# One layer of an mLSTM and convolution trunk: two weight splits moved to VectorE, a norm spread by transfers, another PSUM layout, and edits at both ends

## The chip, the cores and the metric

The kernel runs on one core of a Trainium2 chip. The metric is the device time of one execution in microseconds (us), as the median of three runs. Engines are named as in the profile: PE is TensorE, DVE is VectorE, ACT is ScalarE, POOL is GpSimd, SP is SyncE.

## The reference, cut to what matters

One layer is computed for 128 context tokens and 512 latent tokens of 1024 channels, all in fp32:

```
mod  = silu(cond) @ w_ada + b_ada            # six vectors: shift, scale, gate, twice
h    = rmsnorm(x) * (1 + sc1) + sh1
q, k, v, o, gates, u, ga, gb = split(h @ w_in + b_in)
hA   = bidirectional_mlstm(q, k, v, gates)    # 4 heads, chunks of 128 tokens
branch_a = (sigmoid(o) * norm(hA)) @ w_proj_a
z    = depthwise_conv31(ua * sigmoid(ub))     # 512 channels
branch_b = silu(layernorm(z)) @ w_proj_b      # mean and variance over the 512 channels
x    = x + g1 * ((sigmoid(ga) * branch_a + sigmoid(gb) * branch_b) @ w_out)
h2   = rmsnorm(x) * (1 + sc2) + sh2
gate, val = split(h2 @ w_up)                  # 2 x 2816 columns
x    = x + g2 * ((gelu(depthwise_conv(gate)) * val) @ w_down)
y    = rmsnorm(x)
```

## The kernel before, in words

**Layout.** Channels lie on the 128 partitions and the 640 tokens along a row, so `x` is eight tiles of 128x640. A product with a weight block of 128x128 is done as two matmuls of 320 tokens. An fp32 product is made of three products of a rounded format: weights and activations are each split into a high part and a remainder (`wh`, `wl` for weights; `hh`, `hl` or `ah`, `al` for activations), and TensorE adds wh·hh, wh·hl and wl·hh.

**Weights.** They come in groups of eight blocks, 512 KB each, into a ring of three tiles `wst`, by transfers that SyncE issues. `prep` (line 474) splits a group: ScalarE writes `wh`, and then `wl` comes about in one of two ways. For most groups VectorE computes `wl = wst - wh` (L491). For the groups in the set `TWICE` (line 163) ScalarE writes -`wh` into `wl`, and a transfer issued on GpSimd's queue adds the weights to it from DRAM (L486 to L488). `wh` and `wl` have three tiles each, and from the middle of the up-projection on there is a third ring of three, `wf`.

**Order.** Nothing runs in the order of the text. A planner in the kernel (`_Order`) keeps a cost estimate for every engine and writes one fixed instruction order for each; every instruction is recorded by its helper at line 182 (line 183 in the changed kernel), so the rows of the profile are told apart by tiles. Work is kept in side tasks and in lanes that `od.later` fills and the planner draws from when VectorE seems free: the taps of the convolutions, and the rows `junk`, which compute the six modulation vectors (each multiplies a 128x512 tile `ad` of `w_ada` by the condition, the sum lands in `modp`). `od.need(tag)` writes out at once whatever is left in a lane. The engines run their orders with semaphores between them.

**Stages**, in the order of PE: modulation and first norm; the input projection in the order of `ORDER` (u0 g0 k0 q0 k1 q1 u1 v0 u2 u3 k2 q2 k3 q3 v1 o0 to o3), with the small products of the mLSTM scan, two heads at a time, among them; the two gates and two branch projections in the order of `BRANCH`; the output projection `woA`, `woB`; up- and down-projection; the last norm.

**The convolution's norm** (`conv_norm`, line 1260). When the taps of the four tiles `z` (128x656) are done, 16 products with a tile of ones add up the channels: the sums of the 656 columns come to lie as 4 rows of 164. VectorE scales them to the mean `mu`, `bcast` (line 670) spreads the 4 rows over all partitions with four products `ps<-mu,sel`, VectorE subtracts half a tile at a time, ScalarE squares (`zsq`), 16 more products add up the squares, a short chain on 128x164 gives `rsy`, and `bcast` spreads it by `ps<-rsy,sel`. `conv_out` (line 1294) multiplies and applies the activation; the first branch projection of z is b0.

**PSUM** has eight banks. `psum_pools` (line 393) opens the pool `mm` for the projections and the pool `ps` for small products, anew just before b0 with six banks for `mm` and two for `ps` (line 1397). Tiles of the two are recorded as `mm` and `ps`. In this kernel `mm` then has banks 0 to 5.

**Down-projection and last modulation vector.** In the loop over the tiles f of the up-projection (line 1733) the down-projection runs in parts; a part (`dn_part`, line 1714) has four outputs, and each is added to `x` by VectorE with the gate vector g2 (`x<-mm,mods,x`). Before the first part, at f = 4 (`min(DN_AT)`), stands:

```
        if not wf and (not od.waits("g2") or f == min(DN_AT)):
            od.need("g2")
            g2_in.append(True)
            last.close()
            wf.append(ctx.enter_context(tc.tile_pool(name="wf", bufs=NWF)))
```

`last.close()` frees the tiles `ad`, and `wf` takes their memory: the first ScalarE writes to `wf` wait for the last `junk` to have read.

**The last norm** (`final`, line 1746). The tokens of the second part (256) take squares, sums over channels by products with ones (4 rows of 64 columns), the chain `rsy`, `rsv`, `rst` on 128x64, four spreading products, eight multiplications `yo`, and the last stores.

Of the kernel before, what the change touches and what calls it, by code (L numbers as in the profile page):

```python
# [20 lines left out]
T = NCTX + NLAT  # L21
# [5 lines left out]
TF = 656  # L27
# [49 lines left out]
TL = 384  # L77
# [71 lines left out]
GB = 8  # L149
BLOCKS, HELD, PAIRS = _blocks()  # L150
# [212 lines left out]
def tile_trunk(  # L363
# [17 lines left out]
    od = _Order()  # L381
    V, S, G, PE, Q, GQ = (_Timed(e, od, k) for e, k in ((nc.vector, "V"), (nc.scalar, "S"), (nc.gpsimd, "G"),
                                                        (nc.tensor, "PE"), (nc.sync, "Q"), (nc.gpsimd, "R")))
# [6 lines left out]
    pools = {}  # L390

    def psum_pools(nmm, nps, banks):
        if pools:
            pools["stack"].close()
        pools["stack"] = st = ExitStack()
        pools["nmm"], pools["nps"], pools["banks"] = nmm, nps, banks
        od.rings.clear()
        pools["mm"] = st.enter_context(tc.tile_pool(name=f"mm{nmm}", bufs=nmm, space=bass.MemoryType.PSUM))
        pools["ps"] = st.enter_context(tc.tile_pool(name=f"ps{nps}", bufs=nps, space=bass.MemoryType.PSUM))

    psum_pools(2, 4, 2)
    ctx.enter_context(tc.manual_schedule())
    first, last = ExitStack(), ctx.enter_context(ExitStack())
    adp = first.enter_context(tc.tile_pool(name="adp", bufs=2 * NAD1))

    def A(shape, dt=F32, name="a"):
        return ap.tile(shape, dt, tag="A", name=name)
# [18 lines left out]
    def ps():  # L426
        return od.ring("ps", pools["ps"].tile([P, 512], F32, tag="ps", name="ps"), pools["nps"])
# [2 lines left out]
        return t[:, 0:T].rearrange("p (h n) -> p h n", h=2)  # L430

    HALF = [slice(0, TH), slice(TH, T)]


    cols = cp.tile([P, NCOLS], F32, name="cols")
    sel = cp.tile([P, NSEL], F32, name="sel")
    ident = sel[:, 0:128]
# [15 lines left out]
    lines = {}  # L453
# [17 lines left out]
    def wtile(tag):  # L471
        return od.ring(tag, (wf[0] if tag == "wf" else wp).tile([P, GB * P], F32R, tag=tag, name=tag), CAPS[tag])

    def prep(g, tags=("wh", "wl")):


        if g in ready or g >= NGRP:
            return
        load(g)
        src = stage.pop(g)  # L480
        tag_of["c", g, 0] = tags
        hi, lo = wtile(tags[0]), wtile(tags[1])

        def parts():
            yield from od.until(src)
            S.activation(hi, src, AF.Copy)  # L486
            if g in TWICE:
                S.activation(lo, src, AF.Copy, scale=-1.0)  # L488
                live.pop(g)
                GQ.dma_start(lo, w_d[g], accum_op=ALU.add)  # L490
                return  # L491
            yield
            V.tensor_sub(lo, src, hi.bitcast(F32))
            live.pop(g)

        ready[g] = (hi, lo)
        lines[g] = od.spawn(parts())
# [161 lines left out]
    ones32 = cp.tile([P, 32], F32, name="ones32")  # L659
    V.memset(ones32, 1.0)  # L660
    epsc = cp.tile([P, 1], F32, name="epsc")
    V.memset(epsc, EPS)
    bgrp = T // 4

    def colsum_into(pc, tile_, n, first, last):
# [4 lines left out]
    def bcast(r, n):  # L670
        out = []
        for h in range(2):
            pt = ps()
            for j in range(2):
                g = 2 * h + j
                PE.matmul(pt[:, j * n:(j + 1) * n], lhsT=sel[:, 256 + g:257 + g].to_broadcast([P, P]), rhs=r,
                          start=True, stop=True)
            out.append(pt[:, 0:2 * n])
        return out

    def rstd(src, w, scale, name):

# [17 lines left out]
    x = []  # L700
    for j in range(KD):
        t = A([P, T], name="x")
# [21 lines left out]
    pc = ps()  # L724
    for j in range(KD):
        sq = A([P, T], name="sq")
        S.activation(sq, x[j], AF.Square)
        if j == 3:
            th = small([P, 16], "th")
            S.activation(th, colr("c"), AF.Tanh, scale=0.5)  # L730
            sqrt_table()
        colsum_into(pc, sq, bgrp, j == 0, j == KD - 1)
# [11 lines left out]
    for nm in ("b_ua", "b_ub", "b_o", "mlstm_g", "ln_g", "ln_b", "b_ga", "b_gb"):  # L744
        a, b = _COLS[nm]
# [2 lines left out]
        o += b - a  # L748

    r1 = rstd(pc[:, 0:bgrp], bgrp, 1.0 / D, "rs")  # L750
    prep(0)

    def hcol(name, i):
        return halfc[:, HC[name] + i:HC[name] + i + 1]
# [51 lines left out]
    t_ada = od.spawn(ada1())  # L806
    while not mrows:
        od.finish_one()
    rb = bcast(r1, bgrp)
    t = A([P, T], name="rbs")  # L810
    for h in range(2):
# [40 lines left out]
    z = [None] * 4  # L852
# [91 lines left out]
    for p in range(2):  # L944
        for c in range(NCH):
            t = vp.tile([P, 2, P1], F32, tag="v", name="va")
# [310 lines left out]
    nz = TF // 4  # L1257
    zs = {}

    def conv_norm():  # L1260
        while len(conv_in) < 4 or od.waits("conv"):
            yield
        yield from od.until(*z)
        pc = ps()
        for m in range(4):
            colsum_into(pc, z[m], nz, m == 0, m == 3)
        mu = small([P, nz], "mu")
        V.tensor_scalar(mu, pc[:, 0:nz], 1.0 / 512, None, op0=ALU.mult)
        yield
        mb = bcast(mu, nz)  # L1270
        pc = ps()
        sqs = []
        for m in range(4):
            for h in range(2):
                s = slice(2 * nz * h, 2 * nz * (h + 1))
                V.tensor_sub(z[m][:, s], z[m][:, s], mb[h])
            sq = A([P, TF], name="zsq")
            S.activation(sq, z[m], AF.Square)
            sqs.append(sq)
        for m in range(4):  # L1280
            yield from od.until(sqs[m])
            colsum_into(pc, sqs[m], nz, m == 0, m == 3)
        rz = rstd(pc[:, 0:nz], nz, 1.0 / 512, "rs")
        yield
        rb = bcast(rz, nz)
        ts_ = []
        for m in range(4):
            yield from od.room("V")
            ts_.append(od.spawn(conv_out(m, rb)))
            yield  # L1290
        while not all(t[2] for t in ts_):
            yield

    def conv_out(m, rb):
        for h in range(2):
            s = slice(2 * nz * h, 2 * nz * (h + 1))
            V.tensor_mul(z[m][:, s], z[m][:, s], rb[h])
        yield
        S.activation(z[m], z[m], AF.Identity, scale=hcol("ln_g", m), bias=hcol("ln_b", m))
        yield  # L1300
        t = A([P, TF], name="zt")
        S.activation(t, z[m], AF.Tanh)
        yield
        y = A([P, T], name="zy")
        V.scalar_tensor_tensor(y[:, 0:NCTX], t[:, 0:NCTX], 1.0, z[m][:, 0:NCTX], op0=ALU.add, op1=ALU.mult)
        V.scalar_tensor_tensor(y[:, NCTX:T], t[:, NCTX + PADW:T + PADW], 1.0, z[m][:, NCTX + PADW:T + PADW],
                               op0=ALU.add, op1=ALU.mult)
        hi, lo = zs[m] = A([P, T], F32R, "zh"), A([P, T], F32R, "zl")
        yield
        S.activation(hi, y, AF.Copy)  # L1310
        yield
        V.tensor_sub(lo, y, hi.bitcast(F32))
# [71 lines left out]
    for i, (nm, m) in enumerate(BRANCH):  # L1384
# [9 lines left out]
        else:  # L1394
# [4 lines left out]
            a, b = sgt.pop(("ga", m)), sgt.pop(("gb", m))  # L1399
# [33 lines left out]
    def sums_in(sums, adds, n):  # L1433

        while not all(t[2] for t in adds):
            yield
        pc = ps()
        for i in range(2):
            yield from od.until(sums[i])
            colsum_into(pc, sums[i], n, i == 0, i == 1)  # L1440
        return pc[:, 0:n]

    def bcast_part(r):
        pt = ps()
        n = r.shape[1]
        for g in range(4):
            PE.matmul(pt[:, g * n:(g + 1) * n], lhsT=sel[:, 256 + g:257 + g].to_broadcast([P, P]), rhs=r,
                      start=True, stop=True)
        return pt[:, 0:4 * n]
# [77 lines left out]
    for h in range(2):  # L1527
        sums, adds = [], []
        mat, s = ("woA", "woB")[h], HALF[h]
        pts = [mhalf(mat, m, range(KD - 1), mg, s, last=False) for m in range(2 if h == 0 else 0)]  # L1530
        for m in range(8):
            if m < len(pts):
                pt = mhalf(mat, m, [KD - 1], mg[KD - 1:], s, pt=pts[m], first=False)
# [210 lines left out]

    ks = LASTF

    PARTS = [slice(0, TL), slice(TL, T)]

    def final(h, sums, adds):
        s = PARTS[h]  # L1750
        n = (s.stop - s.start) // 4
        pc = yield from sums_in(sums, adds, n)
        r3 = rstd(pc, n, 1.0 / D, "rs")
        yield
        yield from od.until(r3)
        rb = bcast_part(r3)
        if h == 0:
            for j in range(KD):
                V.scalar_tensor_tensor(x2[j][:, s], x2[j][:, s], col("final_g", j), rb, op0=ALU.mult, op1=ALU.mult)
                Q.dma_start(yT[j, :, s], x2[j][:, s])  # L1760
                yield
            return
        for j in range(0, KD, 2):
            t = A([P, 2, 4 * n], name="yo")
            for i in range(2):
                V.scalar_tensor_tensor(t[:, i, :], x2[j + i][:, s], col("final_g", j + i), rb,
                                       op0=ALU.mult, op1=ALU.mult)
            Q.dma_start(yT[j:j + 2, :, s].rearrange("j p n -> p j n"), t)
# [152 lines left out]
```

## Time and profile before

| | |
|---|---|
| Median of three runs | 950.96 us (949.36 to 951.27) |
| The profiled execution | 950.29 us |
| Its span in the trace | 948.5 us |
| Mean granted TensorE clock | 0.99 |
| PE, DVE, ACT, POOL busy | 96%, 78%, 56%, 14% of the span |

All times in the next part are those of the profiled execution, counted from the start of its span. In a row of the timeline the first number is the start, the second the time, then engine, line, operation and tiles (out<-in), the shape, the number of instructions put together in the row, and in brackets how long the engine had been idle and what it waited for. In a row of windows PEclk is the granted clock as a share of full speed.

### The profile page before, as it was taken

How to read it: one execution, taken by the hardware profiler on the slowest of the kernel's cores; microseconds unless marked ns; L12 is line 12 of the kernel's file. 1: busy time of each engine (PE TensorE's matmuls, PEld its weight loads, DVE VectorE, ACT ScalarE, POOL GpSimd, SP SyncE). 2: the span in 40 equal slices, each digit the busy share in tenths (PEclk: the TensorE clock that was granted, in tenths of full speed). 3: DMA queues.
4: the chain of work that ended last, by engine and by line, in shares of the span. 5: the costliest groups of instructions: out<-in, count | busy, mean ns of one | idle time of the engine just before them, and what ended most of it. 6: DMA issues, size and time to landing. Idle time of an engine off the chain costs nothing.

```text
span 948.5 us, 16981 instructions
## 1 busy us (share of the span) xinstructions
PE 914.2 (96%) x6456; PEld 893.0 (94%) x6456; DVE 742.1 (78%) x1540; ACT 531.6 (56%) x995; POOL 130.6 (14%) x181
## 2 busy tenths in 40 slices
PE   5999997999999999999999999999999999999995
PEld 2899997999999999999999999999999999999995
DVE  3829777887857988889788996877778877878666
ACT  5564575267758222223478766646765666666662
POOL 0001212000000000000000112222222222222210
PEclk9999999899999999999999999999999999999998
DMA  9638939543215646667544769887888889889975
GB/s 356 264 121 170 241 96 264 129 101 89 79 46 166 202 154 196 205 204 257 172 156 133 166 143 201 169 179 169 183 171 183 174 172 183 176 175 185 206 166 150
DMA packets 65954, 164.90 MB, mean 174 GB/s; under 512 B 6864, under 2 KB 15824, under 8 KB 65872
## 3 DMA queue, kind: packets, MB, share of 16 engines
q1 hardware_dynamic: 41360, 113.20, 37.0%
q0 software_dynamic: 24512, 50.60, 31.5%
q8 instruction: 51, 0.84, 0.4%
q14 instruction: 31, 0.25, 0.1%
HBM read 151.39 MB, written 3.48 MB: 163 GB/s over the span
## 4 chain that ended last, share of the span: by engine, by line
PE 83%; DMA 6%; DVE 4%; ACT 3%; issue 2%; SPq 0%; DVEq 0%; POOLq 0%; POOL 0%; ACTq 0%
PE mm L182 64%; PE ps L182 19%; DMA wl<-in_w 2%; DMA E<-in_mask 1%; DMA rowM<-M 1%; DMA out_ocst<-cs 1%; DMA x<-in_xT 1%; ACT L182 1%; DMA E<-rowM 1%; DVE x L182 0%; ACT z L182 0%; SPq L182 0%; DVE wl L182 0%; DMA cb<-in_crow 0%; DVE bc L182 0%
## 5 line engine op out<-in xcount | busy, mean ns | idle before, releaser
L182 ACT ACTIVATE wh<-wst 128x1024 fp32r<-128x1024 f32 (+1 forms) x114 | 114.1, 1007 | 99.2 <-PE mm L182 85.9
L182 DVE SCALAR_TENSOR_TENSOR acc<-gbuf,cols,acc 128x455 f32<-128x455 f32 (+2 forms) x176 | 129.7, 740 | 14.8 <-ACT acc L182 12.4
L182 PE MATMUL mm<-hh,wl 128*128 128x320 f32 (+2 forms) x576 | 134.8, 313 | 5.6 <-DMA wl<-in_w 5.6
L182 PE MATMUL mm<-hh,wh 128*128 128x320 f32 (+2 forms) x576 | 134.3, 312 | 2.9 <-ACT hh L182 1.6
L182 PE MATMUL mm<-hl,wh 128*128 128x320 f32 (+2 forms) x576 | 134.9, 313 | 0.0
L182 DVE SCALAR_TENSOR_TENSOR z<-glu,cols,z 128x641 f32<-128x641 f32 (+14 forms) x120 | 102.4, 887 | 22.6 <-ACT z L182 21.6
L182 POOL DMA_DIRECT2D wl<-in_w x69 | 60.9, 883 | 390.3 <-ACT wl L182 225.5
L182 PEld LDWEIGHTS mm<-hh,wl 128*128 128x128 f32 x576 | 97.0, 190 | 7.1 <-DMA wl<-in_w 5.9
L182 PEld LDWEIGHTS mm<-hh,wh 128*128 128x128 f32 x576 | 97.7, 190 | 4.8 <-ACT hh L182 2.1
L182 PEld LDWEIGHTS mm<-hl,wh 128*128 128x128 f32 x576 | 97.1, 190 | 1.8 <-issue 1.3
L182 PE MATMUL mm<-h,wh 128*128 128x320 f32 x452 | 85.5, 310 | 1.4 <-ACT h L182 0.8
L182 DVE SCALAR_TENSOR_TENSOR junk<-ad,cb 128x512 bf16<-128x512 f32 x128 | 82.0, 685 | 0.0
L182 DVE TENSOR_TENSOR wl<-wst,wh 128x1024 fp32r<-128x1024 f32 x55 | 67.1, 1221 | 17.2 <-ACT wh L182 17.1
L182 PE MATMUL mm<-al,wh 128*128 128x320 f32 (+2 forms) x336 | 80.5, 309 | 0.0
L182 PE MATMUL mm<-ah,wh 128*128 128x320 f32 (+2 forms) x336 | 80.3, 309 | 0.0
L182 PE MATMUL mm<-ah,wl 128*128 128x320 f32 (+2 forms) x336 | 80.3, 308 | 0.0
L182 ACT ACTIVATE wl<-wst 128x1024 fp32r<-128x1024 f32 (+1 forms) x91 | 74.3, 840 | 4.7 <-PE mm L182 4.7
L182 PEld LDWEIGHTS mm<-h,wh 128*128 128x128 f32 x452 | 71.2, 188 | 2.7 <-DVE h L182 1.2
L182 PE MATMUL mm<-h,wl 128*128 128x320 f32 x364 | 73.1, 309 | 0.3 <-DMA wl<-in_w 0.3
L182 DVE SCALAR_TENSOR_TENSOR x<-mm,mods,x 128x128 f32<-128x128 f32 (+1 forms) x168 | 63.7, 433 | 8.1 <-PE mm L182 7.5
L182 PEld LDWEIGHTS mm<-h,wl 128*128 128x128 f32 x364 | 58.5, 188 | 0.6 <-DMA wl<-in_w 0.6
L182 PEld LDWEIGHTS mm<-ah,wh 128*128 128x128 f32 x336 | 57.2, 188 | 0.1
(249 smaller groups left out, 1930.6 us busy)
## 6 DMA issues: line engine op xcount, KB each, us to landing
wst<-in_w SPq DMA_DIRECT2D x138, 512.0 KB, 4.5
wl<-in_w POOLq DMA_DIRECT2D x47, 512.0 KB, 7.2
ad<-in_ada SPq DMA_DIRECT2D x64, 256.0 KB, 3.1
adst<-in_ada SPq DMA_DIRECT2D x16, 512.0 KB, 10.2
wf<-in_w POOLq DMA_DIRECT2D x23, 256.0 KB, 5.0
wh<-sf POOLq DMA_DIRECT2D x22, 256.0 KB, 5.3
wl<-in_w POOLq DMA_DIRECT2D x22, 256.0 KB, 6.0
x<-in_xT SPq DMA_DIRECT2D x16, 320.0 KB, 5.8
```

The source lines that it names most:

```text
L182: return fn(*args, **kw)
```

## The change

1. The groups of k2 and q2 leave `TWICE`: their `wl` is computed by VectorE from `wst` and `wh`, and two accumulating transfers are gone from GpSimd's queue.
2. `psum_pools` with six and two banks opens `ps` first: `ps` has banks 0 and 1, `mm` 2 to 7.
3. At the start four of eight squares go from ScalarE to VectorE, the table change on ScalarE comes one square earlier, and the first weight group is split after the first modulation row and not before it.
4. `conv_norm` spreads mean and rstd by transfers: the 4 rows of 164 are written to DRAM and read back to all partitions as a tile `zb` of 128x656 (`on_all`), both issued by SyncE. VectorE then works on whole tiles in SBUF.
5. In `final` for the last 256 tokens the sums are made with the squares as weights, so that the tokens come to lie on the partitions: the chain has 2 columns in place of 64, and two products of 128 columns with `ident` turn and spread it. The first part of the sums no longer waits for the last addition.

```
+TWICE -= {_g for _g in _IN if BLOCKS[_g * GB][0] in ("k", "q") and BLOCKS[_g * GB][2] == 2}
...
-        pools["mm"] = st.enter_context(tc.tile_pool(name=f"mm{nmm}", bufs=nmm, space=bass.MemoryType.PSUM))
-        pools["ps"] = st.enter_context(tc.tile_pool(name=f"ps{nps}", bufs=nps, space=bass.MemoryType.PSUM))
+        for nm, n in (("mm", nmm), ("ps", nps))[::-1 if banks == 1 else 1]:
+            pools[nm] = st.enter_context(tc.tile_pool(name=f"{nm}{n}", bufs=n, space=bass.MemoryType.PSUM))
...
-        S.activation(sq, x[j], AF.Square)
-        if j == 3:
+        if j in (3, 4, 5, 7):
+            V.tensor_mul(sq, x[j], x[j])
+        else:
+            S.activation(sq, x[j], AF.Square)
+        if j == 2:
...
+    def on_all(r):
+
+        d = dz.tile([4, nz], F32, tag="row", name="zrow")
+        Q.dma_start(d, r[0:P:32, :])
+        t = A([P, TF], name="zb")
+        Q.dma_start(t, d.rearrange("g n -> (g n)").unsqueeze(0).to_broadcast([P, TF]))
+        return t
...
-        mb = bcast(mu, nz)
+        mb = on_all(mu)
...
-            for h in range(2):
-                s = slice(2 * nz * h, 2 * nz * (h + 1))
-                V.tensor_sub(z[m][:, s], z[m][:, s], mb[h])
+            yield from od.until(mb)
+            V.tensor_sub(z[m], z[m], mb)
...
-        rb = bcast(rz, nz)
+        rb = on_all(rz)
+        yield from od.until(rb)
...
+            token_sums(pc, sums[0], n * P, True, False)
+            while not adds[-1][2]:
+                yield
+            yield from od.until(sums[1])
+            token_sums(pc, sums[1], n * P, False, True)
...
-        rb = bcast_part(r3)
+        rb = bcast_part(r3) if h == 0 else token_rows(r3, 0, n)
```

The planner writes all orders anew, so instructions also move where no line was changed. Three places follow. In a row of an order x6 means six such instructions in a row.

VectorE during k2, where it runs taps (`z<-glu,cols,z`) and the gated product `glu`; before:

```order
L182 SCALAR_TENSOR_TENSOR glu<-gt,gy 128x512
L182 SCALAR_TENSOR_TENSOR z<-glu,cols,z 128x652
L182 SCALAR_TENSOR_TENSOR z<-glu,cols,z 128x653
L182 SCALAR_TENSOR_TENSOR z<-glu,cols,z 128x641
L182 SCALAR_TENSOR_TENSOR z<-glu,cols,z 128x654
L182 SCALAR_TENSOR_TENSOR z<-glu,cols,z 128x642
L182 SCALAR_TENSOR_TENSOR z<-glu,cols,z 128x655
```

and in the changed kernel:

```order
L183 SCALAR_TENSOR_TENSOR glu<-gt,gy 128x512
L183 TENSOR_TENSOR wl<-wst,wh 128x1024
L183 SCALAR_TENSOR_TENSOR z<-glu,cols,z 128x652
L183 SCALAR_TENSOR_TENSOR z<-glu,cols,z 128x653
L183 SCALAR_TENSOR_TENSOR z<-glu,cols,z 128x641
L183 SCALAR_TENSOR_TENSOR z<-glu,cols,z 128x654
L183 SCALAR_TENSOR_TENSOR z<-glu,cols,z 128x642
L183 TENSOR_TENSOR wl<-wst,wh 128x1024
L183 SCALAR_TENSOR_TENSOR z<-glu,cols,z 128x655
```

The two splits, of k2 and of q2, stand among the taps; nothing else is moved here.

VectorE around f = 4, with `acc` the taps of the up-projection's convolution, `sf` sums of weight blocks, `mods` the end of the modulation, and `x_4744` or `x_4712` the first of the tiles that the down-projection adds to; before, where the last `junk` stands twelve rows ahead of that addition:

```order
L182 SCALAR_TENSOR_TENSOR junk,modp<-ad,cb 128x512
L182 TENSOR_TENSOR mods<-modp 128x16
L182 TENSOR_TENSOR mods<-mods,cols 128x16
L182 TENSOR_TENSOR al<-ge,ah 128x640
L182 TENSOR_TENSOR sf<-wst 128x512
L182 SCALAR_TENSOR_TENSOR acc<-gbuf_5603,cols,acc 128x648 x2
L182 SCALAR_TENSOR_TENSOR acc<-gbuf_5603,cols,acc 128x455
L182 TENSOR_TENSOR wl<-sf,wl 128x512
L182 SCALAR_TENSOR_TENSOR acc<-gbuf_5603,cols,acc 128x455 x4
L182 TENSOR_TENSOR sf<-sf,wst 128x512
L182 TENSOR_TENSOR sf<-wst 128x512
L182 TENSOR_TENSOR sf<-wst,sf 128x512
```

and in the changed kernel, from the same taps on:

```order
L183 SCALAR_TENSOR_TENSOR acc<-gbuf_5569,cols,acc 128x455 x4
L183 SCALAR_TENSOR_TENSOR acc<-gbuf_5569,cols,acc 128x454
L183 SCALAR_TENSOR_TENSOR junk,modp<-ad,cb 128x512 x6
L183 TENSOR_TENSOR mods<-modp 128x16
L183 TENSOR_TENSOR mods<-mods,cols 128x16
L183 TENSOR_TENSOR sf<-sf,wst 128x512
L183 TENSOR_TENSOR sf<-wst 128x512
L183 TENSOR_TENSOR sf<-wst,sf 128x512
L183 SCALAR_TENSOR_TENSOR x_4712<-mm,mods,x_4712 128x128
L183 SCALAR_TENSOR_TENSOR x_4712<-mm,mods,x_4712 128x192
L183 SCALAR_TENSOR_TENSOR x_4712<-mm,mods,x_4712 128x320
L183 TENSOR_TENSOR ge<-ge,mm 128x320 x2
```

Six `junk` and the two `mods` that stood ahead of the taps, or earlier, now stand behind them, and directly ahead of what the down-projection waits for.

SyncE's transfers around the norm, with `zrow` the rows in DRAM; in the changed kernel:

```order
L183 DMA wst<-in_w 128x1024 x5
L183 DMA zrow<-mu 4x164
L183 DMA zb<-zrow 128x656
L183 DMA wst<-in_w 128x1024 x2
L183 DMA zrow<-rsy 4x164
L183 DMA zb<-zrow 128x656
L183 DMA cb<-in_crow 128x512 x4
```

Before, the seven loads `wst` and the four `cb` follow each other there; now two loads stand behind the first pair and the `cb` behind the second.

More of the change, by code (lines that the diff above doesn't have):

```diff
@@ L432, in tile_trunk @@
     HALF = [slice(0, TH), slice(TH, T)]
+    PARTS = [slice(0, TL), slice(TL, T)]
     cols = cp.tile([P, NCOLS], F32, name="cols")
@@ L472, in wtile, with prep @@
         return od.ring(tag, (wf[0] if tag == "wf" else wp).tile([P, GB * P], F32R, tag=tag, name=tag), CAPS[tag])
-    def prep(g, tags=("wh", "wl")):
+    def prep(g, tags=("wh", "wl"), wait=True):
         if g in ready or g >= NGRP:
@@ L484, in parts @@
         def parts():
-            yield from od.until(src)
+            if wait:
+                yield from od.until(src)
             S.activation(hi, src, AF.Copy)
@@ L679, in bcast, with token_sums, token_rows @@
         return out
+    def token_sums(pc, tile_, w, first, last):
+        n = w // P
+        for c in range(n):
+            PE.matmul(pc[:, c:c + 1], lhsT=tile_[:, c * P:(c + 1) * P], rhs=ones32[:, 0:1], start=first and c == 0,
+                      stop=last and c == n - 1)
+    def token_rows(r, a, b):
+        pt = ps()
+        for c in range(a, b):
+            PE.matmul(pt[:, (c - a) * P:(c - a + 1) * P], lhsT=r[:, c:c + 1].to_broadcast([P, P]), rhs=ident,
+                      start=True, stop=True)
+        return pt[:, 0:(b - a) * P]
     def rstd(src, w, scale, name):
@@ L750, in tile_trunk @@
     r1 = rstd(pc[:, 0:bgrp], bgrp, 1.0 / D, "rs")
-    prep(0)
     def hcol(name, i):
@@ L808, in tile_trunk @@
         od.finish_one()
+    prep(0, wait=False)
+    od.force(lines[0])
     rb = bcast(r1, bgrp)
@@ L1258, in tile_trunk @@
     zs = {}
+    dz = ctx.enter_context(tc.tile_pool(name="dz", bufs=2, space=bass.MemoryType.DRAM))
+    def on_all(r):
[4 more added lines that the diff above has]
+        return t
     def conv_norm():
@@ L1294, in conv_out @@
     def conv_out(m, rb):
-        for h in range(2):
-            s = slice(2 * nz * h, 2 * nz * (h + 1))
-            V.tensor_mul(z[m][:, s], z[m][:, s], rb[h])
+        V.tensor_mul(z[m], z[m], rb)
         yield
@@ L1745, in tile_trunk @@
     ks = LASTF
-    PARTS = [slice(0, TL), slice(TL, T)]
     def final(h, sums, adds):
         s = PARTS[h]
-        n = (s.stop - s.start) // 4
-        pc = yield from sums_in(sums, adds, n)
+        if h == 0:
+            n = (s.stop - s.start) // 4
+            pc = yield from sums_in(sums, adds, n)
+        else:
+            n = (s.stop - s.start) // P
+            while not all(t[2] for t in adds[:-1]):
+                yield
+            yield from od.until(sums[0])
+            pc = ps()
+            token_sums(pc, sums[0], n * P, True, False)
+            while not adds[-1][2]:
+                yield
+            yield from od.until(sums[1])
+            token_sums(pc, sums[1], n * P, False, True)
+            pc = pc[:, 0:n]
         r3 = rstd(pc, n, 1.0 / D, "rs")
@@ L1763, in final @@
         for j in range(0, KD, 2):
-            t = A([P, 2, 4 * n], name="yo")
+            t = A([P, 2, n * P], name="yo")
             for i in range(2):
```

## The prediction

> **What bounds the kernel now.** The page's busy times and its chain of waits come first.
>
> ```profile
> PE 914.2 (96%) x6456; PEld 893.0 (94%) x6456; DVE 742.1 (78%) x1540; ACT 531.6 (56%) x995; POOL 130.6 (14%) x181
> ...
> PE 83%; DMA 6%; DVE 4%; ACT 3%; issue 2%; SPq 0%; DVEq 0%; POOLq 0%; POOL 0%; ACTq 0%
> ...
> L182 PE MATMUL mm<-hh,wl 128*128 128x320 f32 (+2 forms) x576 | 134.8, 313 | 5.6 <-DMA wl<-in_w 5.6
> ```
>
> TensorE is busy for 914.2 of the span's 948.5 us, so an edit counts for what PE does in it or waits for; 34 us of idle time are all there is. The third row, from the costliest groups, shows a single wait of 5.6 us for a transfer of `wl`. The timeline of PE has its place, and the windows of 10 us (PE, weight loads, DVE, ACT, POOL, granted clock, DMA share, GB/s) what it leaves behind.
>
> ```profile
> 166.35 0.90 PE L182 MATMUL mm<-hh,wl 128*128 128x320 f32 x2 [5.63 <-DMA wl<-in_w]
> ...
> 171.31 0.46 PE L182 MATMUL mm<-hh,wl 128*128 128x320 f32 x2
> 171.60 0.46 PE L182 MATMUL mm<-hh,wh 128*128 128x320 f32 x2
> ```
>
> ```profile
> 160.00:170.00 10.00, 4.37 (x19) 4.11 (x19) 10.00 (x15) 2.68 (x3) 0.86 (x1) 0.72 1.10 261
> 170.00:180.00 10.00, 10.00 (x66) 10.00 (x66) 10.00 (x13) 2.69 (x3) 0.86 (x1) 0.94 0.17 33
> ```
>
> PE stops for 5.63 us, and then runs at a low clock (0.72 and 0.94 in the means): from 166.35 to 171.31 nine pairs of matmuls pass in 4.96 us, where a pair takes 0.29 at full clock (171.31 to 171.60), 2.6 us for nine. So 2.3 us more are lost, 7.9 in all. Most of the other idle time lies at the two ends, where PE waits for short chains of other engines.
>
> **The change part by part.** *The splits of k2 and q2.* Why the transfer was late is in the timelines of ScalarE and GpSimd.
>
> ```profile
> 148.10 1.05 ACT L182 ACTIVATE wl<-wst 128x1024 fp32r<-128x1024 f32 x1
> ```
>
> ```profile
> 148.51 1.56 POOL L182 DMA_DIRECT2D E<-in_mask  x1 [7.14 <-DVE z L182]
> 152.56 1.55 POOL L182 DMA_DIRECT2D E<-in_mask  x1 [2.49 <-DMA E<-rowM]
> 153.53 1.59 POOL L182 DMA_DIRECT2D wl<-in_w  x1
> ...
> 163.15 0.86 POOL L182 DMA_DIRECT2D wl<-in_w  x1 [4.03 <-ACT wl L182]
> ```
>
> ```profile
> L182 DVE TENSOR_TENSOR wl<-wst,wh 128x1024 fp32r<-128x1024 f32 x55 | 67.1, 1221 | 17.2 <-ACT wh L182 17.1
> ```
>
> ScalarE's part of k2 was done at 149.1, but the issue stood in GpSimd's queue behind two mask transfers and left at 153.53; the data came when PE went on, 12.8 us later. VectorE's split takes 1.22 us and stands right behind the gated product, so k2's `wl` is there at about 150.5, ten us early. q2's stands five taps later, near 159, and is wanted seven us after k2 begins. Next in line is k3, whose transfer left at 163.15. A group is 24 pairs, 7.0 us; with the stop gone k2 begins at 160.7 and PE wants k3 near 174.7, 11.6 us after that issue, with two 512 KB transfers fewer on the way. I take the whole stop as gone: −7.9.
>
> VectorE pays 2 x 1.22 = 2.4 us for it, and what it does behind (taps, then the second scan's tiles) comes later against PE. The cover is its next idle stretch:
>
> ```profile
> 192.92 3.30 DVE L182 SCALAR_TENSOR_TENSOR z<-glu,cols,z 128x641 f32<-128x641 f32 x4 [7.62 <-ACT z L182]
> ```
>
> 7.62 us, three times the price, but PE gains 7.9 there and the stretch shrinks to nearly nothing, so that some lateness remains for the scan behind it. Between 0 and 2.4 I take +0.7.
>
> *The convolution's norm.* PE loses both spreads:
>
> ```profile
> 267.28 1.28 PE L182 MATMUL ps<-mu,sel 128*128 128x164 f32 x8
> ...
> 271.71 0.49 PE L182 MATMUL ps<-zsq,ones 128*32 128x164 f32 x8
> ...
> 282.79 1.27 PE L182 MATMUL ps<-rsy,sel 128*128 128x164 f32 x8
> ```
>
> −2.55. In their place come a small write to DRAM and a read to 128 partitions (336 KB). The transfers (median us to landing last) and the window:
>
> ```profile
> E<-rowM SPq DMA_DIRECT2D x8, 256.0 KB, 7.3
> ...
> out_yT<-x SPq DMA_DIRECT2D x8, 192.0 KB, 1.9
> cb<-in_crow SPq DMA_DIRECT2D x4, 256.0 KB, 3.8
> ...
> out_om<-me SPq DMA_DIRECT2D x1, 0.2 KB, 8.6
> ```
>
> ```profile
> 270.00:280.00 10.00, 10.00 (x86) 8.19 (x85) 2.83 (x7) 6.63 (x10) 0.00 (x0) 1.00 0.12 46
> ```
>
> No such pair is in the trace. Its nearest rows are the stores (1.9 us to landing) and the condition row `cb`, also one DRAM row read to all partitions (3.8), both on quiet engines, as here: DMA share 0.12. The far ends are `out_om` (8.6) and `E` (7.3), issued under load. So the round trip takes 5.7, at most 15.9 us. PE does not wait for it until it wants the squares' sums: from the mean's spread to these the trace has 4.43 us (267.28 to 271.71), and the new order puts 30 pairs of matmuls, 8.8 us, and three transposes between. Around the round trip lie the scaling, the first subtraction (0.8 for 656 columns, by the split's 1.22 for 1024), the first square (as much) and the steps between the engines; I give them 2.6 us, and 5.7 + 2.6 = 8.3 is under 9. Nothing is added. The second spread has its reader only in b0, over 40 us on.
>
> *PSUM.* The wait at b0 stays, I think:
>
> ```profile
> 336.10 0.54 PE L182 MATMUL mm<-zh,wh 128*128 128x320 f32 x2 [1.01 <-DVE ga L182]
> ```
>
> The pool's first tile still lies in banks that the branch projection before it used, and its first matmul waits for the same reader: 0, at best −1.0.
>
> *The start.* ScalarE's last four squares wait for nothing there:
>
> ```profile
> 9.77 2.60 ACT L182 ACTIVATE sq<-x 128x640 f32<-128x640 f32 x4
> ```
>
> They end at 12.4; by VectorE the last ends when x has come, 0.2 to 0.4 earlier; then PE is held by the loads of the modulation weights. 0.
>
> *The end.*
>
> ```profile
> 938.59 0.54 DVE L182 RECIPROCAL rsy<-rsy 128x64 f32<-128x64 f32 x1
> ```
>
> ```profile
> 140.25 0.17 DVE L182 RECIPROCAL rd<-rd 128x2 f32<-128x2 f32 x1
> ```
>
> ```profile
> 940.06 1.94 PE L182 MATMUL ps<-rsy,sel 128*128 128x64 f32 x8 [2.02 <-DVE rsy L182]
> ```
>
> On 2 columns the reciprocal costs 0.17 and not 0.54, and the four short rows beside it should save a little each: −0.5 to −0.6 together. The spread takes 1.94 for four products of 64 columns with four weight loads; two of 128 columns move as many columns with half the loads, so they take between half and all of it; I take 1.2, nearer to the half, since loads are most of such small products. Sums with the squares as weights cost 0.1 to 0.4 more. −1.0, between −0.5 and −1.5, all on the path, since only the multiplications and stores follow.
>
> *What the new order adds at f = 4.* Six rows `junk` that were spread over the time before are written out at once, between the taps and the additions to `x`. In the trace of before:
>
> ```profile
> 559.07 0.69 DVE L182 SCALAR_TENSOR_TENSOR junk<-ad,cb 128x512 bf16<-128x512 f32 x1
> 559.68 0.08 DVE L182 DVE_READ_ACCUMULATOR junk<-ad,cb 128x1 f32 x1
> 559.80 0.17 DVE L182 TENSOR_TENSOR mods<-modp 128x16 f32<-128x16 f32 x1
> ...
> 568.74 0.69 DVE L182 TENSOR_TENSOR sf<-sf,wst 128x512 f32<-128x512 f32 x1
> ...
> 570.73 1.14 DVE L182 SCALAR_TENSOR_TENSOR x<-mm,mods,x 128x128 f32<-128x128 f32 x3
> ...
> 572.38 0.69 DVE L182 SCALAR_TENSOR_TENSOR acc<-gbuf,cols,acc 128x454 f32<-128x454 f32 x1
> ```
>
> ```profile
> 571.55 0.45 PE L182 MATMUL mm<-ah,wh 128*128 128x320 f32 x2
> ```
>
> The down-projection's third output starts at 571.55, in the banks that the first held until VectorE had read them at 570.73 and on: no wait, and no slack. In the new order, behind the taps that end at 568.74, come one more tap (0.6, the row at 572.38 with the overlap off), six `junk` at 0.61 (the step from 559.07 to 559.68), 3.7, `mods` at 0.4 (two of 0.17 and the step ahead of them), and the three `sf` that stood there already, 2.0 (568.74 to 570.73). The additions begin at 568.74 + 0.6 + 3.7 + 0.4 + 2.0 = 575.4, and PE needs their first half, 0.6 more: 576.0 against 571.55, a wait of 4.4 us. ScalarE's first writes to `wf`, which wait for the last `junk`, come late by as much; their readers then are late already. Then there is the clock.
>
> ```profile
> 112.69 0.38 PE L182 MATMUL mm<-wh,hh 128*128 128x256 f32 x1 [2.15 <-DVE va L182]
> ```
>
> ```profile
> 114.00:116.00 2.00, 2.00 (x11) 2.00 (x11) 2.00 (x5) 1.67 (x6) 0.00 (x0) 0.50 1.08 207
> 116.00:118.00 2.00, 2.00 (x17) 2.00 (x16) 1.81 (x4) 2.00 (x8) 0.00 (x0) 0.83 0.19 35
> ```
>
> Even behind a wait of 2.15 us the clock fell to 0.50; the mean of 0.83 in the next two says that it lasted 0.7 us more, so 2.7 us and what lies ahead of 114 went at half the pace, a loss of 1.4 to 1.6. Behind 5.63 us it was 2.3. For 4.4 us I take 1.9: in all +6.3, between 0 and 8.
>
> [...]
>
> **The sum**: −7.9 + 0.7 − 2.55 − 1.0 + 6.3 = −4.45. Against the profiled execution's 950.29 that is 945.8; the median, 950.96, lies 0.67 higher, and against it 946.5. I forecast 946.2, between.
>
> **The rivals.** *The six rows are covered* (VectorE gets to f = 4 earlier, since it has done six fewer by then). Against it: VectorE waited 1.37 us for ScalarE ahead of these taps, which hang on PE's own output, so an early VectorE would wait longer. For it: the trace of before cannot show where VectorE then stands. 946.2 − 6.3 = 939.9.
>
> ```profile
> 562.88 2.55 DVE L182 SCALAR_TENSOR_TENSOR acc<-gbuf,cols,acc 128x648 f32<-128x648 f32 x3 [1.37 <-ACT acc L182]
> ```
>
> *Slower: the round trip through DRAM is late.* PE would stand at the squares' sums. It has about 6.4 us for the two transfers (9 less 2.6); each us more is a us of waiting, and from some 2 us of wait the clock's 1.6 to 2.3 come too. The whole is slower than before by over 0.2% when wait and clock exceed 4.8 + 1.9 = 6.7, at a round trip of some 11 us; at the far end of 15.9 it is 9.5 + 2 more, about 957.5. The low DMA share speaks against it, `out_om` for it.
>
> *Part of the stop stays*: the splits wait in VectorE's order for ScalarE or behind taps, k3's transfer is late in turn, or the scan of the second pair of heads is late by the 2.4 us and the clock falls there. Half of the 7.9 would be given back: 946.2 + 4 = 950.2. The change then does little of what it says.
>
> **How the numbers follow.** Forecast 0.50, covered 0.20, late round trip 0.13, stop stays in part 0.17. About 0.2% (1.9 us) is what a measurement of this kernel can tell from no change. Faster by more: the first two, and 0.06 of the rest, 0.76; within it 0.14 (most of the fourth, little of the third); slower 0.10. The likeliest case's own range is 944 to 948.5. To hold eight in ten I go from 939.5, which leaves out half of the covered case, to 951.5, which leaves out most of the late round trip.
>
> **What would show it.** Right: no wait on PE for `wl` near 160 and a clock of 1.00 there; no `ps<-mu,sel` and `ps<-rsy,sel` at 128x164; no wait ahead of the first `zsq` sums; a wait on PE of 4 to 5 us for DVE `x` near 560 with a low clock behind it; a last spread of about 1.2 us; the wait for `ga` at b0 still 1 us. Wrong: no such wait behind the six `junk` (then it is 940), a wait for `zsq` (then slower), or a new stop between 175 and 235.

## The result, and the profile after

The changed kernel takes 943.91 us (median of four runs, 942.54 to 945.95), the kernel before 950.25 on the same chip: a ratio of 0.9935, with a 95% interval of 0.9912 to 0.9957. The forecast was 946.2, with a range of 939.5 to 951.5. The profiled execution is the slowest of the four, 945.95 us with a span of 944.2; its busy times and the chain that ended last:

```profile
PE 913.5 (97%) x6428; PEld 890.2 (94%) x6428; DVE 747.2 (79%) x1538; ACT 527.5 (56%) x989; POOL 128.8 (14%) x179
...
PE 83%; DMA 6%; DVE 5%; issue 3%; ACT 2%; SPq 1%; POOL 0%; DVEq 0%; POOLq 0%; ACTq 0%
```

TensorE is about as busy as before (914.2), with 28 recorded matmuls fewer; its idle time went from 34.3 to 30.7 us. Since nearly every matmul stands in both traces, the starts of the same matmul say where time was won and lost (us from the start of the span; between 200 and 299 small products change places, and the row there goes by the projections alone):

| the same matmul | before | after | after minus before |
|---|---|---|---|
| first of the projections | 20.57 | 22.48 | +1.9 |
| end of the first two units | 56.77 | 58.68 | +1.9 |
| in v0, after its wait | 116.92 | 117.94 | +1.0 |
| first that needs k2's `wl` | 166.35 | 161.67 | −4.7 |
| in q2, at full clock again | 181.41 | 174.41 | −7.0 |
| ahead of the norm's sums | 255.68 | 248.42 | −7.3 |
| behind the norm's spreads | 299.64 | 289.31 | −10.3 |
| up-projection | 511.06 | 500.72 | −10.3 |
| a late transfer of `wl` | 526.21 | 516.94 | −9.3 |
| f = 4, just ahead of the third output | 571.41 | 561.93 | −9.5 |
| behind f = 4 | 593.97 | 590.23 | −3.7 |
| near the end | 926.60 | 923.00 | −3.6 |
| end of the span | 948.5 | 944.2 | −4.3 |

**k2.** The windows of the changed kernel at the same place:

```profile
160.00:170.00 10.00, 10.00 (x70) 10.00 (x69) 10.00 (x14) 4.38 (x6) 0.89 (x1) 1.00 0.87 186
170.00:180.00 10.00, 10.00 (x71) 10.00 (x70) 10.00 (x13) 3.70 (x5) 1.72 (x2) 1.00 0.59 125
```

PE is busy throughout at a clock of 1.00. VectorE's two splits and its taps in the timeline:

```profile
150.05 1.22 DVE L183 TENSOR_TENSOR wl<-wst,wh 128x1024 fp32r<-128x1024 f32 x1
...
158.75 1.22 DVE L183 TENSOR_TENSOR wl<-wst,wh 128x1024 fp32r<-128x1024 f32 x1
...
175.20 21.11 DVE L183 SCALAR_TENSOR_TENSOR z<-glu,cols,z 128x647 f32<-128x647 f32 x26
```

They end at 151.3 and 160.0, long ahead of their use. The idle stretch of 7.62 us that VectorE had at 185 is gone: 26 taps follow each other, and PE waits for none of it.

**The norm.** SyncE's two transfers, VectorE's subtraction and the first sums of squares in the timeline, and the transfers' group:

```profile
260.90 0.57 SPq L183 DMA_DIRECT2D zrow<-mu  x1
262.56 0.33 SPq L183 DMA_DIRECT2D zb<-zrow  x1
...
267.88 3.09 DVE L183 TENSOR_TENSOR z<-z,zb 128x656 f32<-128x656 f32 x4
...
270.00 0.48 PE L183 MATMUL ps<-zsq,ones 128*32 128x164 f32 x8
```

```profile
zb<-zrow SPq DMA_DIRECT2D x2, 328.0 KB, 3.6
```

The write takes 1.66 us (to the issue of the read, which waits for it), the read 3.6: 5.3 for the round trip. VectorE had other work until 267.88, and the sums of squares start with no wait.

**f = 4.** VectorE, ScalarE and PE in the timeline:

```profile
560.00 0.69 DVE L183 SCALAR_TENSOR_TENSOR junk<-ad,cb 128x512 bf16<-128x512 f32 x1
...
563.79 0.17 DVE L183 TENSOR_TENSOR mods<-modp 128x16 f32<-128x16 f32 x1
...
565.90 1.13 DVE L183 SCALAR_TENSOR_TENSOR x<-mm,mods,x 128x128 f32<-128x128 f32 x3
...
563.79 2.19 ACT L183 ACTIVATE wf<-wst 128x512 fp32r<-128x512 f32 x4 [8.85 <-DVE junk L183]
...
568.56 1.13 ACT L183 ACTIVATE wf<-sf 128x512 fp32r<-128x512 f32 x2
...
566.72 0.78 PE L183 MATMUL mm<-ah,wh 128*128 128x320 f32 x2 [2.71 <-DVE x L183]
...
574.98 1.73 PE L183 MATMUL ps<-hx,wf 128*128 128x320 f32 x10 [0.66 <-DMA wf<-sf]
```

```profile
566.00:568.00 2.00, 1.28 (x5) 1.11 (x6) 2.00 (x6) 0.79 (x3) 0.96 (x2) 0.85 0.50 82
568.00:570.00 2.00, 2.00 (x10) 2.00 (x9) 1.60 (x4) 2.00 (x4) 0.02 (x1) 0.50 0.92 264
570.00:572.00 2.00, 2.00 (x13) 2.00 (x13) 1.35 (x2) 2.00 (x4) 1.30 (x2) 0.80 1.02 339
```

The six `junk` run from 560.00 to 563.7, the additions to `x` begin at 565.90, PE stops for 2.71 us and then runs at a clock of 0.50, and it waits 0.66 us more for `wf`: 5.7 us in all by the table (from −9.5 to −3.7), more than half of what had been won by then.

### The profile page after: what moved, and what is told of

It is laid out like the page before. It is cut to its first block, busy times and chain, and to the rows that moved or that the text cites. A ratio compares the mean times of both kernels' runs of the same rounds, so it can differ in the third digit from the quotient of the medians.

```text
span 944.2 us, 16922 instructions
## 1 busy us (share of the span) xinstructions
PE 913.5 (97%) x6428; PEld 890.2 (94%) x6428; DVE 747.2 (79%) x1538; ACT 527.5 (56%) x989; POOL 128.8 (14%) x179
## 4 chain that ended last, share of the span: by engine, by line
PE 83%; DMA 6%; DVE 5%; issue 3%; ACT 2%; SPq 1%; POOL 0%; DVEq 0%; POOLq 0%; ACTq 0%
PE mm L183 64%; PE ps L183 19%; DMA wl<-in_w 2%; DMA E<-in_mask 1%; DMA rowM<-M 1%; SPq L183 1%; DMA x<-in_xT 1%; DMA ad<-in_ada 1%; DVE junk L183 1%; DMA wf<-sf 1%; DMA E<-rowM 1%; DVE acc L183 0%; DVE x L183 0%; DVE wl L183 0%; DVE sq L183 0%
## 5 line engine op out<-in xcount | busy, mean ns | idle before, releaser
L183 POOL DMA_DIRECT2D wl<-in_w x67 | 58.5, 873 | 381.6 <-ACT wl L183 202.9
L183 DVE TENSOR_TENSOR wl<-wst,wh 128x1024 fp32r<-128x1024 f32 x57 | 69.6, 1221 | 17.8 <-ACT wh L183 17.7
L183 ACT ACTIVATE wl<-wst 128x1024 fp32r<-128x1024 f32 (+1 forms) x89 | 72.2, 835 | 4.7 <-PE mm L183 4.7
```

Source lines behind the costliest of these rows:

```text
L183: return fn(*args, **kw)
```

## The experiments

Each kernel was timed against the kernel before on the same chip in one session; a ratio under 1 is faster. Experiments 1 to 4 share one session, 5 to 8 a second, 9 to 11 a third.

**1. The splits alone.** The kernel before with one line added:

```
+TWICE -= {_g for _g in _IN if BLOCKS[_g * GB][0] in ("k", "q") and BLOCKS[_g * GB][2] == 2}
```

> Only the splits of k2 and q2 are moved to VectorE; the rest is the kernel before, and the planner's order has no burst of junk at f = 4. My theory (the stop of 5.6 us and the low clock behind it both go, VectorE's 2.4 us are hidden): 8 us faster, about 942.3, no wait on PE for wl near 160. Rival (part of the stop stays, or the second scan is late by VectorE's 2.4 us): 4 to 5.5 us faster, about 945, with a new wait on PE between 175 and 235.

941.80 us against 949.93, ratio 0.9932 (0.9917 to 0.9947). Its trace has no wait near 160, and by matching matmuls its lead grows from 0.1 us at 155 to 8.2 at 206. The whole stop went, and the single line is worth more than the change as a whole in the same session (experiment 4).

**2. The norm alone.** The kernel before with `on_all` as in the change, and:

```
-        mb = bcast(mu, nz)
+        mb = on_all(mu)
...
-        rb = bcast(rz, nz)
+        rb = on_all(rz)
+        yield from od.until(rb)
...
+        V.tensor_mul(z[m], z[m], rb)
```

> Only the convolution norm's spread by transfers. The planner's order now leaves seven junk for f = 4, one more than in the changed kernel. My theory (two spreads are worth 2.6 to 3.1 us, the burst costs about 6): slower than the kernel before by 3 to 4 us, about 953.5, with a wait on PE for x behind the junk and a low clock. Rival (the burst comes from elsewhere, or is covered): 3 us faster, about 947.2.

952.55 us, ratio 1.0033 (1.0012 to 1.0054): slower by 2.6 us, a little less than the 3 to 4 of the first theory. Its lead over the kernel before changes by +6.1 us at f = 4 (from 1.5 ahead to 4.6 behind). PE there:

```profile
575.29 0.78 PE L182 MATMUL mm<-ah,wh 128*128 128x320 f32 x2 [3.32 <-DVE x L182]
...
583.44 1.72 PE L182 MATMUL ps<-hx,wf 128*128 128x320 f32 x10 [0.56 <-DMA wf<-sf]
```

Seven `junk` in place of six, 3.32 us of wait in place of 2.71: one `junk` (0.61) more. So this edit brings the burst by itself.

**3. The changed kernel with the old start.** Undone are the squares, the place of the table change and `prep(0)`:

```
-        if j in (3, 4, 5, 7):
-            V.tensor_mul(sq, x[j], x[j])
-        else:
-            S.activation(sq, x[j], AF.Square)
-        if j == 2:
+        S.activation(sq, x[j], AF.Square)
+        if j == 3:
...
+    prep(0)
...
-    prep(0, wait=False)
-    od.force(lines[0])
```

> The changed kernel with the start of the kernel before. In this order the planner draws the junk in time and f = 4 has no burst. My theory (the burst costs 5.7 us, the start's edit is worth nothing): 8.1 + 3.1 + 0.7 under the kernel before, about 938.4. Rival (the burst cost little by itself, other things were late at f = 4): 943 to 944, as the changed kernel. If the start's edit was worth something, it is that much above 938.4.

944.54 us, ratio 0.9945 (0.9924 to 0.9965). The expectation rested on a misreading: this order has the same six `junk` at f = 4, and its trace the same wait (2.69 us for `x`) and the same step (+5.8 by matching matmuls). What it does tell is the start's price: against experiment 4, the same with the new start, its median is 1.8 us lower, though single executions of the two overlap.

**4. The changed kernel again**, with no edit.

> The changed kernel once more, unchanged. Its first profile began the projections 1.9 us later than the kernel before, with the small products of the start at half pace, and it was 2 us above its median. If this is the start's edit, the profile shows it again; if it is the phase of one execution, the projections begin within 0.5 us of 20.6 and the time is about 943.5.

946.34 us, ratio 0.9966 (0.9946 to 0.9985). The projections begin at 22.92, again late. Over the two measurements the change gains 3.6 to 6.3 us. At f = 4 the repeat has the six `junk` and the same wait, but the clock stays at 1.00 behind it:

```profile
565.75 0.78 PE L183 MATMUL mm<-ah,wh 128*128 128x320 f32 x2 [2.71 <-DVE x L183]
```

```profile
566.00:568.00 2.00, 2.00 (x14) 1.88 (x14) 2.00 (x7) 1.05 (x2) 0.17 (x1) 1.00 0.95 160
```

It falls to 0.50 only at 574.7, behind two more waits (1.09 us for ScalarE, 0.70 for `wf`), and the step comes to 7.1 us where the first profile had 5.7.

**5. The burst spread.** The changed kernel, with a few lines ahead of `ffn_tile(f)`:

```
+    def draw(n):
+        outer, od.line, od.filling = od.line, None, True
+        for _ in range(n):
+            if od.waits("g2"):
+                od.bg[20].pop(0)[1]()
...
     for f in range(2, NF):
+        draw({2: 4, 3: 4}.get(f, 0))
         ffn_tile(f)
```

> The changed kernel with one thing more: four junk each are drawn ahead of f = 2 and f = 3, so that none is left over for f = 4. My theory (the six junk at f = 4 cost 5.7 us): about 5.7 us under the changed kernel, 938 to 940 where that shows 944 to 946, and at 555 to 580 no wait on PE of over 0.5 us. Rival (VectorE has no room anywhere there, so the time is only moved): a new wait of PE for VectorE between 520 and 560, and the changed kernel's time within 2 us.

941.96 us, ratio 0.9920 (0.9890 to 0.9951), against 944 to 946 for the changed kernel in the other sessions: 2 to 4.4 us gained, less than the 5.7 expected. The trace says why: a wait for `x` is left, half as long and with the clock at 1.00 behind it.

```profile
565.07 0.78 PE L183 MATMUL mm<-ah,wh 128*128 128x320 f32 x2 [1.37 <-DVE x L183]
```

No `junk` is left for f = 4, but the end of the modulation (`mods`) is, and `od.need` draws the lane of taps ahead of the lane of `junk`: all taps of the tile still come ahead of the additions.

**6. The same with the old start**: the edits of 5 and 3 together.

> As the kernel with the burst spread, with the start of the kernel before. If the start's edit costs something, this one is 1 to 2 us faster than that; if its late start was the phase of single executions, the two agree within 1 us, and over several executions both begin the projections about equally.

940.30 us, ratio 0.9903 (0.9870 to 0.9936); by matching matmuls it leads experiment 5 by 0.95 us at the first projection and by 0.8 to 1.2 from there to the end. With experiments 3 and 4 this is the second pair in which the new start costs 1 to 2 us by the medians (1.7 here, 1.8 there).

**7. The end alone.** The kernel before with `token_sums` and `token_rows`, used in `final` for the second part as in the change:

```
+            token_sums(pc, sums[0], n * P, True, False)
...
+            token_sums(pc, sums[1], n * P, False, True)
...
-        rb = bcast_part(r3)
+        rb = bcast_part(r3) if h == 0 else token_rows(r3, 0, n)
```

> Only the last norm is changed. My theory: 0.7 us faster by the trace (the short chain from the last product to the end of the span is 12.0 us in place of 12.7), 949.3 where the kernel before shows 950. Rival (the stores set the end): no difference in that stretch.

947.37 us, ratio 0.9981 (0.9968 to 0.9995). From the last product to the end of the span it has 11.5 us, the kernel before 12.7, the changed kernel 11.9 (11.6 in the repeat). The medians differ by 2.7 us, more than the 0.7 expected and more than the 1.2 that this stretch shows; in the trace another 1.0 us is gained ahead of it, where the edit changes nothing, so not all of the 2.7 is the edit's.

**8. The start alone.** The kernel before with the edit of 3 the other way round, its `-` and `+` exchanged.

> Only the start is changed: four squares on VectorE, the table change one square earlier, the first split after the first modulation row. If the start's edit costs what the two profiles of the changed kernel showed, the projections begin near 22.5 in place of 20.6 and the time is 1 to 2 us above the kernel before. If that was the phase of single executions, it is within 0.5 us of the kernel before.

950.91 us, ratio 1.0013 (0.9996 to 1.0029): by itself the interval just holds no change. Its projections begin late too:

```profile
16.27 2.50 PE L182 MATMUL ps<-rsy,sel 128*128 128x160 f32 x8 [0.64 <-DVE rsy L182]
...
22.93 0.56 PE L182 MATMUL mm<-hh,wh 128*128 128x256 f32 x2 [1.59 <-ACT hh L182]
```

Over all thirteen traces, the old start has its first projection at 20.1 to 20.6 (four times), or at 21.8 to 22.3 (five times, with the spread `ps<-rsy,sel` at 2.50 us in place of 1.35); the new one at 22.5 to 22.9, with 2.50, in all four. A late start thus occurs without the edit too; against the late ones the new start is 0.7 us later in the mean, against all nine of the old start 1.4. Whether the edit also makes the late start more frequent (four of four against five of nine) the counts do not settle.

**9. Drawn ahead of f = 4.** As 6, so that nothing is left for `need`:

```
-        draw({2: 4, 3: 4}.get(f, 0))
+        draw({2: 4, 3: 6}.get(f, 0))
```

> As the kernel with the burst spread and the old start, but four junk are drawn ahead of f = 2 and six ahead of f = 3, so that nothing is left to be forced at f = 4; the taps and the modulation's end then stand again as in the kernel before. My theory (there, need wrote out the taps as well, ahead of the additions to x, and 1.2 us of wait and its clock stayed): the rest of the step at f = 4, some 2.3 us, goes too, about 938, and PE waits under 0.3 us for x. Rival (the extra VectorE work at f = 2 and 3 is itself the cost): a wait of PE on ScalarE or VectorE between 515 and 545, and no gain.

938.53 us, ratio 0.9878 (0.9838 to 0.9918), the fastest median of the eleven with that of experiment 11. PE no longer waits for `x`; of the step at f = 4 some 0.5 us are left, 0.25 of them the second of these waits:

```profile
521.22 1.04 PE L183 MATMUL mm<-h,wh 128*128 128x320 f32 x4 [1.27 <-ACT gbuf L183]
...
568.06 1.72 PE L183 MATMUL ps<-hx,wf 128*128 128x320 f32 x10 [0.25 <-DMA wf<-sf]
```

The first row is the rival's share: with the ten `junk` drawn at f = 2 and 3 PE waits 1.27 us there, where the kernel before has no such wait. Both theories hold a part, the first the larger.

**10. The mean by two round trips.** Experiment 9 with one more trip, and the order of all other engines kept:

```
+        q0 = od.free["Q"]
+        hop = small([P, nz], "hop")
+        dh = dz.tile([4, nz], F32, tag="row", name="zrow")
+        Q.dma_start(dh, mu[0:P:32, :])
+        V.memset(hop, 0.0)
+        Q.dma_start(hop[0:P:32, :], dh)
+        od.free["Q"], od.ready[hop.tensor.name] = q0, od.ready[mu.tensor.name]
-        mb = on_all(mu)
+        mb = on_all(hop)
```

> As the kernel with the junk drawn before f = 4, but the mean goes to DRAM and back to its four rows once more before it is spread, with every instruction of the other engines left in its place in the order. The mean then comes about 4 us later than the 5.3 us that one round trip took in the changed kernel. My theory (there are about 2 us to spare between the spread mean and the first sums of squares): PE waits about 2 us there, and with the clock behind it the time is 2 to 4 us above the kernel with one round trip. Rival (there is much more to spare, and the norm was never near PE's path): no wait for zsq, and the same time within 0.7 us.

942.18 us, ratio 0.9914 (0.9880 to 0.9948), 3.7 above experiment 9. The timeline:

```profile
260.60 0.58 SPq L183 DMA_DIRECT2D zrow<-mu  x1
262.35 0.52 SPq L183 DMA_DIRECT2D hop<-zrow  x1
264.08 0.48 SPq L183 DMA_DIRECT2D zrow<-hop  x1
265.69 0.33 SPq L183 DMA_DIRECT2D zb<-zrow  x1
...
269.65 3.10 DVE L183 TENSOR_TENSOR z<-z,zb 128x656 f32<-128x656 f32 x4 [2.00 <-DMA zb<-zrow]
...
271.33 0.48 PE L183 MATMUL ps<-zsq,ones 128*32 128x164 f32 x8 [1.56 <-ACT zsq L183]
```

The mean comes 3.4 us later (its spread is issued 5.09 us behind the first write, 1.65 in experiment 9) and PE waits 1.56: about 1.8 us were to spare. By matching matmuls the wait costs 1.6 us; behind 1.56 us the clock did not fall. The other 2 of the 3.7 us are not shown to be the trip's. In the trace 1.5 us arise at 191, ahead of the norm, where PE waits 1.28 us for a transfer of `wl`, and 0.7 at f = 4, where it waits 0.93 us for `wf` (0.25 in experiment 9). That the total fell within the 2 to 4 us expected is thus in part luck.

**11. The PSUM order undone.** Experiment 9 with `mm` opened first again:

```
-        for nm, n in (("mm", nmm), ("ps", nps))[::-1 if banks == 1 else 1]:
+        for nm, n in (("mm", nmm), ("ps", nps)):
```

> As the kernel with the junk drawn before f = 4, with the PSUM pools in the order of the kernel before. My theory (the first product of b0 waits for the same reader in both layouts): the same time within 0.7 us, and the wait of 1.0 us for ga at b0 in both. Rival (the layout saves a wait elsewhere): 1 us or more slower.

939.43 us, ratio 0.9879 (0.9844 to 0.9913): 0.9 us above experiment 9 by the medians, where 0.7 was the bound set, but with overlapping executions (937.15 to 939.68 against 938.28 to 939.69). The first product of b0 waits as before, here with the old layout, and in the changed kernel with the new one:

```profile
324.66 0.53 PE L183 MATMUL mm<-zh,wh 128*128 128x320 f32 x2 [1.00 <-DVE ga L183]
```

```profile
325.63 0.53 PE L183 MATMUL mm<-zh,wh 128*128 128x320 f32 x2 [1.00 <-DVE ga L183]
```

## Why the prediction was right, and where it was not

**The sum: right, in part by luck.** The profiled pair differs by −4.35 us where the sum had −4.45. Three things that the sum counted at nothing (+1.9 at the start, −0.9 at v0, +1.0 for a late transfer at 517) come to +2.0, and its own terms came out 2.0 us better than forecast, above all VectorE's lateness, the norm and f = 4.

**The splits: right.** −7.9 forecast; −8.0 by matching matmuls (from +1.0 to −7.0), −8.1 alone. The +0.7 for VectorE's lateness did not come: between 181 and 256 the lead even grows by 0.3, and no wait there is for the taps. There is a new wait between 175 and 235, which the prediction had named as a sign of being wrong, but it is for a transfer of `wl` (0.52 us at 192.65) and costs 0.8 us; it is not in the traces of experiments 1 and 9. The 0.95 us that PE waited at 225.41 in the kernel before are gone, which makes up for it.

**The norm: right, by a margin of 1.8 us.** −2.55 forecast, −3.1 measured between 256 and 300 (0.0 between the same matmuls of experiment 1, which has no edit of the norm); the 0.41 us that PE had waited at 299.64 went as well. The round trip took 5.3 us (5.7 forecast), and experiment 10 shows the rival's mechanism, a late round trip, with the threshold near where the sum had it: 9 less 2.6 is 6.4 us for the transfers, 5.3 + 1.8 = 7.1 measured.

**f = 4: the size right in part by luck, one step wrong.** +6.3 forecast, +5.7 measured. VectorE's side came as worked out: the additions begin at 565.90, which is 575.4 less the lead of 9.5. The step that failed is "PE needs their first half … a wait of 4.4 us": in the changed kernel the third output runs without a wait from 562.1, 3.8 us ahead of the first addition, so it needs no bank that these free; it is the fourth that waits, 2.71 us. The wait comes to 2.9 us by the table's way of counting and not 4.4, the clock to 2.0 (1.9 forecast); what filled the sum up again was the 0.66 us for `wf`, whose readers I had called "late already" and counted at nothing. That this wait stems from the burst is not shown: with no `junk` left there, PE waits for `wf` 0.65 us at the same place in experiment 1 and 0.93 in experiment 10, and with the burst not at all in experiment 3. Nor is the low clock directly behind the wait certain: the repeat had none there. The rival (the rows are covered) is out: experiments 2, 5 and 9 change the place of the `junk`, and with it the wait. That they come late at all stems from the norm's edit (experiment 2; the traces of the splits, the start and the end alone have two there, done by 560, as the kernel before has, and PE does not wait for `x`). At the matmul that both traces have near 320 us of before, 13 `junk` are done before and 6 after, and the difference stays until f = 4. Why the planner draws fewer there was not tried.

**The start: wrong.** 0 forecast; +1.7 and +1.8 by the medians of two pairs of kernels, +0.9 alone (−0.4 to +2.8). The step was "then PE is held by the loads of the modulation weights": the squares do end earlier (9.48 for the last run of sums and not 10.54), but PE's small products then run at about half pace (2.50 us for the spread below, 1.35 in the kernel before) and the first split comes behind them. The trace's record of the clock has its rise to full at 21.3 us here and at 14.3 in the kernel before. Which of the three edits costs it was not tried.

```profile
9.48 3.18 PE L183 MATMUL ps<-sq,ones 128*32 128x160 f32 x32 [0.66 <-DVE sq L183]
...
15.67 2.50 PE L183 MATMUL ps<-rsy,sel 128*128 128x160 f32 x8 [0.62 <-DVE rsy L183]
...
22.48 0.55 PE L183 MATMUL mm<-hh,wh 128*128 128x256 f32 x2 [1.59 <-ACT hh L183]
```

**The end: right in kind.** −1.0 forecast, −0.8 in the profiled pair, −1.1 in the repeat, −1.2 in experiment 7. The rows:

```profile
934.12 0.60 PE L183 MATMUL ps<-ones,sq 128*128 128x1 f32 x4 [0.17 <-ACT sq L183]
...
935.13 0.15 DVE L183 RECIPROCAL rsy<-rsy 128x2 f32<-128x2 f32 x1
...
936.02 1.19 PE L183 MATMUL ps<-sel,rsy 128*128 128x128 f32 x4 [1.30 <-DVE rsy L183]
```

The spread took 1.19 (1.2 forecast) and the reciprocal 0.15 in place of 0.54; the sums with the squares as weights 0.60 in place of 0.32. In both spreads weight loads are busy for most of the time, 1.78 of the 1.94 us before and 0.92 of the 1.19 after, at a clock of 0.50 in both.

**PSUM: right**, 0 in two layouts. Not foreseen: a wait of 1.42 us for a transfer of `wl` at 516.94, 0.33 before; it is smaller or absent in other traces (1.04, 0.62, 0.52, and none in the repeat of the same kernel), so it belongs to the execution.

## What to carry to other kernels

An edit that removes work from the busiest engine can pay for it hundreds of us later, where a planner draws its background work by slack: compare the orders at every place where a leftover is forced, and time each part by itself, since here one of the five parts was worth as much as all of them together, or more. A wait of a few us on the matrix engine is to be priced with the low clock that may follow, which cost 2.0 to 2.3 us behind waits of 2.7 and 5.6, though a second execution with the wait of 2.7 was spared it there. The broadcast through DRAM, 5.3 us, cost PE no wait while it lay beside other products, and 1.56 us of wait when its mean came 3.4 us later (experiment 10): count the matmuls that the order puts between its start and its first reader.

## What the runs showed of the hardware

**Waits and the clock.** Behind 2.15 us (before, v0) the clock fell to 0.50; behind 2.22 us at the same place of the changed kernel it did not:

```profile
115.23 0.39 PE L183 MATMUL mm<-wh,hh 128*128 128x256 f32 x1 [2.22 <-DVE va L183]
```

```profile
116.00:118.00 2.00, 2.00 (x19) 2.00 (x18) 2.00 (x4) 1.83 (x7) 0.00 (x0) 1.00 1.18 214
```

That is the 0.9 us that the changed kernel wins between 57 and 117. Waits of 1.37 (experiment 5) and 1.56 us (experiment 10) left the clock at 1.00. In the wait of 5.63 us it fell to 0.50 (before, from 164.45 to 171.28), and behind 5.10 and 5.54 at the same place a pair of matmuls took 0.53 us in place of 0.29 (experiments 7 and 8). The 2.71 us at f = 4 lowered it in the first profile and not in the repeat. So the length of a wait alone does not decide. In the traces of before and after the stretches between two recorded changes of the clock are whole multiples of 3.41 us (before: 99.0, 3.4, 47.8, 6.8 and 768.0; after: 546.1, 3.4 and 365.2). Counted in stretches of 3.41 us from these changes, the wait of 2.15 us lies in one of them (before), the 2.22 us across two of them (after, first row), the 2.71 us in one (after, second row), and the repeat's 2.71 us across two (the figure behind the length is PE's busy time):

```profile
109.84:113.25 3.41, 1.26 (x11) 1.06 (x10) 2.44 (x4) 1.22 (x3) 0.00 (x0) 1.00 1.39 197
```

```profile
113.42:116.84 3.42, 1.61 (x13) 1.61 (x14) 3.42 (x6) 1.47 (x5) 0.00 (x0) 1.00 1.42 194
563.98:567.39 3.41, 0.70 (x4) 0.50 (x4) 3.39 (x9) 2.72 (x6) 1.73 (x2) 1.00 0.14 22
```

```profile
561.02:564.43 3.41, 2.02 (x14) 1.75 (x12) 3.34 (x11) 1.60 (x4) 0.16 (x1) 1.00 0.00 0
564.43:567.84 3.41, 2.09 (x13) 1.91 (x13) 3.41 (x10) 2.20 (x6) 1.57 (x2) 1.00 0.56 86
```

The clock fell at the end of the stretches in which PE was busy for 1.26 and 0.70 us, and not behind those with 1.61, 2.02 and 2.09. Five stretches show no bound, and no experiment was made for one.

**Half pace under a clock of 1.00.** At the start the spread of 8 recorded matmuls takes 1.35 us in four of the thirteen traces and 2.50 in nine, while the granted clock in the windows from 15 to 18 reads 1.00 in both kinds (1.35 in the kernel before, 2.50 in the changed one). The column says nothing yet at that time: the record of the clock begins with the rise to full, at 14.3 us in the trace of before, ahead of the spread (16.19), and at 21.3 in that of after, behind it (15.67). All four traces of the new start have 2.50, and their first projection is 2.3 us later in the mean than in the four with 1.35, all of the old start. What makes the rise early or late is not shown.

**A row through DRAM.** 2.6 KB from four partitions to DRAM took 1.6 to 1.8 us until the next transfer was issued (1.66 and 1.67 in the changed kernel, 1.75 and 1.61 in experiment 10), the way back to four partitions as long (1.73, experiment 10), and the read to 128 partitions (328 KB) 3.6 (the changed kernel).
